# A transformer layer on one core: the output projection in one written order, its first unit and a quarter of the next inside the last attention unit, weights and operands in one pool of 4 KB tiles

## The chip, the core and the metric

The kernel runs on one core of one Trainium2 chip. The metric is the time of one execution in microseconds (us) of the device. The instructions run on five engines: TensorE (PE in the profile, with its weight loads as PEld), VectorE (DVE), ScalarE (ACT), GpSimd (POOL) and SyncE (SP), which here issues DMA transfers only.

## The reference

One layer works on 2048 tokens of 1024 features. In all projections, H = 16 heads of 64 features: 8 heads of forgetting attention ("fox") and 8 of stick-breaking attention ("sb").

```python
h = rms_norm(x, g_attn) * (1 + scale_a) + shift_a        # scale, shift, gate from silu(c) @ w_ada + b_ada
q_f, k_f, v_f, q_s, k_s, v_s, f_logit = split(h @ w_in)
o_fox = forgetting_attention(q_f, k_f, v_f, log_sigmoid(f_logit + b_fgate))
o_sb  = stick_breaking_attention(q_s, k_s, v_s)
mix = concat([head_rms_norm(o_fox, g_out_fox), head_rms_norm(o_sb, g_out_sb)])
x = x + gate_a * (mix @ w_out)                           # the output projection
h = rms_norm(x, g_mlp) * (1 + scale_m) + shift_m
u = causal_depthwise_conv(h @ w_up, conv_w, conv_b)      # the channel mixer
u_gate, u_val = split(u)
x = x + gate_m * ((silu(u_gate) * u_val) @ w_down)
return rms_norm(x, g_final)
```

`head_rms_norm` divides each head's 64 outputs of a token by their root mean square. All is float32 for the outside; the change concerns the line marked "output projection", the norm behind it, and the step into the channel mixer.

## The kernel before

**Products.** A float32 operand is split into a high and a low part (`split`: ScalarE copies the high part, L44; VectorE or GpSimd subtracts to get the low part, L45). Each product takes three matmuls, high by high, high by low, low by high.

**Attention.** It runs over 32 units (8 head pairs by 4 blocks `tb` of 512 tokens). Each unit writes its outputs, not yet normalised, to memory as `os_[p][tb]` (128 features of a head pair by 512 tokens), and the squares' sums of the heads to `var[tb]`. `interleave` puts steps of other work (the projections of later units, and `tail` in the last unit) between the steps of the unit at hand.

**Who sets the order.** A scheduler in the compiler orders each engine's instructions by its own model of their times. Two means override it: `tc.issue_after(ins)` keeps the instructions of a block behind one instruction, and `fixed()` keeps them, on every engine that it touches (the DMA issues of SyncE too), behind the last instruction of the block before, so that a chain of such blocks runs in the order in which it is written. In the output projection before, neither is used.

**Row scales.** `head_scale(tb)` takes the root and the reciprocal of `var[tb]`, transposes them on TensorE and stores them as `rstd[tb]`: one row of 512 tokens for each of the 16 heads.

**Output projection.** It runs in eight units `u` of 256 tokens (`HT`). For each of the 8 head pairs `p`, `make_mix` loads `o` (128 by 256) from `os_`, and `r`: the two rows of `rstd` that belong to the pair, each repeated to 64 partitions, by two DMAs of 64 KB (L877). GpSimd multiplies them (L880), and `split` makes the mix tile. I call this a blend. `out_proj` then computes, for each tile `t` of 128 tokens and each half `n` of the 1024 output columns, 8 × 3 = 24 matmuls (L895), adds the residual rows of `x` (L899) and stores the sum as `x1s` (L900). `finish_out` normalises the unit's two row tiles (L983), transposes them in eight steps of two (L987), applies scale and shift on ScalarE (L989) and stores the result `hf_m`, 64 DMAs of 128 KB in all, from ScalarE's queue into `hms` (L991).

Unit 0's matmuls are mixed into the last attention unit (`first_mix`, `first_out`), its sum goes to memory and is read back in the loop over `u`, which handles all units, each with the blends of the next ahead of it.

**Channel mixer.** `h_operands` reads `hms` for half of the tokens (`sblk`, 1024 tokens) in four steps `j`, and builds seven operands for a form of the product with seven multiplications in place of eight. `ob{j}` and `oa{j}` hold three and four of them in one tile each. `w_operands` does the same for the weights, and `pair_first` computes the first column tile of a token half with `j` as the outer loop, 4 × 7 × 3 = 84 matmuls (L1084); `pair` and a last piece (`REST`) follow. The whole is done for `sblk` 0, then 1; the place between them is called the change of token half. Then comes the down projection.

Of the kernel before, what the change touches and what calls it, by code (L numbers as in the profile page):

```python
# [8 lines left out]
F32 = mybir.dt.float32  # L9
# [24 lines left out]
def kernel(ctx: ExitStack, tc: tile.TileContext, x, c, w_ada, b_ada, g_attn, w_in, b_fgate,  # L34
# [17 lines left out]
    hms = [[dram.tile([P, 2 * TB], F32, name=f"hm{s}_{k}") for k in range(KT)] for s in range(2)]  # L52
# [542 lines left out]
    def weighted(o, kts, blk, V, hl, first, last, diag):  # L595
# [11 lines left out]
        for kk, kt in enumerate(kts):  # L607
            for w in range(2):
                rhs = at[:, w].rearrange("p (s q) -> p s q", q=P)[:, 0:4:3, :] if kk else at[:, w, P:3 * P]
                nc.tensor.matmul(o[:, 0:2 * P], V[kt // 4][:, kt % 4, hl, :], rhs,  # L610
                                 start=first and kk == 0 and w == 0, stop=last and kk == 1 and w == 1)
# [66 lines left out]

    deferred = []
# [8 lines left out]
    def attend(kind, p, tb, res, Fbs):  # L688
# [3 lines left out]
        oT = sb.tile([P, TB], F32, name="oT", bufs=2)  # L692
        if kind == "fox":
            ls = sx.tile([P, 2, 4], F32, name="ls", bufs=2)
        mp = p if kind == "fox" else p + 4

        def head_var(j2):
# [5 lines left out]
            def reduce():  # L703
                b = pt()
# [150 lines left out]
    HT = 2 * P  # L855

    def head_scale(tb, b, pool):
        v = var[tb].rearrange("p t h -> p (t h)")
        nc.scalar.activation(v, v, AF.Sqrt)
        nc.vector.reciprocal(v, v)  # L860
        nc.tensor.transpose(b[0:8 * NPAIR, 0:P], v, ident)
        r = pool.tile([8 * NPAIR, P], F32, name="rs", bufs=1)
# [4 lines left out]
    def load_o(u, p):  # L867
        o = p2a.tile([P, HT], F32, name="o", bufs=3)
        nc.sync.dma_start(o, os_[p][u // 2][:, (u % 2) * HT:(u % 2 + 1) * HT])
        return o  # L870

    def make_mix(u, mix, pool, loaded=()):
        for p in range(NPAIR):
            o = loaded.pop(0) if loaded else load_o(u, p)
            r = p2a.tile([P, HT], F32, name="r", bufs=2)
            for h in range(2):
                nc.sync.dma_start(r[h * HD:(h + 1) * HD],  # L877
                                  rstd[u // 2][2 * p + h:2 * p + h + 1,
                                               (u % 2) * HT:(u % 2 + 1) * HT].to_broadcast([HD, HT]))
            nc.gpsimd.tensor_mul(o, o, r)  # L880
            m = pool.tile([P, 2, HT], F32R, name="mix", bufs=8)
            split(m[:, 0], m[:, 1], o, nc.vector)
            mix.append(m)
            yield

    def out_proj(u, mix, x1_tile, acc_bank, xts):
        for t in range(2):
            row = u * HT + t * P
            xt = x1_tile()
            nc.sync.dma_start(xt, x[row:row + P, :])  # L890
            for n in range(2):
                b = acc_bank()
                for p in range(NPAIR):
                    for i, (a, bb) in enumerate(((0, 0), (0, 1), (1, 0))):
                        nc.tensor.matmul(b, mix[p][:, a, t * P:(t + 1) * P], wo[p][:, bb, n * 512:(n + 1) * 512],  # L895
                                         start=p == 0 and i == 0, stop=p == NPAIR - 1 and i == 2)
                    if p % 2:
                        yield
                nc.vector.tensor_add(xt[:, n * 512:(n + 1) * 512], b, xt[:, n * 512:(n + 1) * 512])  # L899
            nc.sync.dma_start(x1s[row // P], xt)  # L900
            xts.append(xt)
        yield

    mix0 = []

    def first_mix(loaded):
        mix = mix0
        for kt, _ in enumerate(make_mix(0, mix, p2a, loaded)):
            w = p2a.tile([P, 2, D], F32R, name=f"wo{kt}")
            nc.sync.dma_start(f(w), wos[kt])  # L910
            wo.append(w)
            yield

    def first_out():
        pair = sx.tile([P, S], F32, name="p", bufs=4)
        halves = [pair[:, :D], pair[:, D:]]
        yield from out_proj(0, mix0, lambda: halves.pop(0), lambda: bank(psc, "bc", 2), [])
# [9 lines left out]
    tail = None  # L927
    for i, u in enumerate(units):
# [12 lines left out]
        if i >= len(units) - 2:  # L941
            head_scale(i - len(units) + 2, pt(), sx)
        if nxt is None:
# [3 lines left out]
            p2a = open_pool("p2a")  # L947
            loaded = [load_o(0, p) for p in range(3)]
            wo = []
            tail = first_mix(loaded)  # L950
# [11 lines left out]
        interleave(attend(kind, p, tb, results[kind, p], Fbs), n, [(lm if i >= LATE else None, PER, False), (tail, 12, True)], follow)  # L962
# [3 lines left out]
    drain(first_out())  # L966
    tick(1 << 20)
    for t in range(2, NTB):
        head_scale(t, bank(psc, "bc", 2), p2a)
    close_pool("fx", "px", "sb", "psb")  # L970
# [4 lines left out]
    p2b = open_pool("p2b")  # L975

    NU = S // HT

    def finish_out(u, xts):
        sl = slice(u % 4 * HT, (u % 4 + 1) * HT)  # L980
        r = rms_scale(p2b, xts, "m")
        for i, xt in enumerate(xts):
            nc.vector.tensor_scalar_mul(xt, xt, r[:, i:i + 1])  # L983
        for kt in range(KT):
            ps = bank(psd, "t", 2)
            for i, xt in enumerate(xts):
                nc.tensor.transpose(ps[:, i * P:(i + 1) * P], xt[:, kt * P:(kt + 1) * P], ident)  # L987
            hf = p2b.tile([P, HT], F32, name="hf_m", bufs=2)
            nc.scalar.activation(hf, ps[:, :HT], AF.Identity, scale=mod_m[:, 0, kt:kt + 1],  # L989
                                 bias=mod_m[:, 1, kt:kt + 1])  # L990
            nc.scalar.dma_start(hms[u // 4][kt][:, sl], hf)  # L991

    def x1_tile():
        return p2b.tile([P, D], F32, name="x1", bufs=4)

    mixes = {}
    for u in range(NU):
        if u + 1 < NU:
            mixes[u + 1] = []
            drain(make_mix(u + 1, mixes[u + 1], p2b if u % 2 == 0 else p2a))  # L1000
        xts = []
        if u:
            drain(out_proj(u, mixes[u], x1_tile, lambda: bank(psd, "o", 4), xts))
        else:
            for t in range(2):
                xts.append(x1_tile())
                nc.sync.dma_start(xts[t], x1s[t])
        finish_out(u, xts)
    close_pool("p2b", "p2a")

    ho1 = open_pool("hop1")
    up_ = open_pool("up")
    NK = KT // 2
    SB = 2 * TB

    def bank_a():
        return bank(psd, "o", 4)

    def bank_c():
        return bank(psd, "t", 2)  # L1020

    obs = {}

    def h_operands(sblk, j):

        pool = ho if j == 0 else ho1
        xh = ho.tile([P, 2, SB], F32, name="xh", bufs=2)
        for i in range(2):
            nc.sync.dma_start(xh[:, i], hms[sblk][j + i * NK])
# [265 lines left out]
```

## Time and profile before

| quantity | value |
|---|---|
| median of 3 runs | 3072.32 us (3069.5 to 3076.95) |
| the profiled execution | 3060.69 us |
| its span in the profile | 3059.0 us |
| TensorE's mean granted clock in it | 0.985 of full speed |
| TensorE busy | 2950.6 us, 96% of the span, 16012 matmuls and transposes |
| VectorE, ScalarE, GpSimd busy | 2085.6, 1687.9, 969.1 us |
| DMA | 546.79 MB in 302677 packets |

The span is the time from the first to the last record of the profiled execution, which took 1.69 us more than its span. A busy time is the sum of an engine's instructions, not a measure of how well it is used. "PEclk" is the clock that the throttle granted to TensorE in a stretch (1.00 is full). In a stretch's row each engine's busy time is followed by its count of instructions. In the waits, an engine's operation stands left, what it waited for right of the arrow, then the sum of that idle time, how many waits, and the longest. L numbers are lines of the kernel.

### The profile page before, as it was taken

The page shows a single profiled execution, that of the slowest core. Times are in us where ns is not written, and L with a number is a line of the kernel's source. Part 1 is how long each engine was busy: PE and PEld are TensorE (multiplying, and loading weights), DVE is VectorE, ACT ScalarE, POOL GpSimd, SP SyncE. Part 2 cuts the span into 40 slices and gives each one's busy share as a digit, 9 for nine tenths or more (in the row PEclk, how much of TensorE's full clock was granted, in tenths as well). Part 3 has the DMA queues.
Part 4 walks back from the last instruction along what each step waited for, and adds up shares of the span by engine and source line. Part 5 has one row for each costly group of instructions (what it writes and reads, how often), then busy time and mean ns, then how long its engine had stood idle before and what let it go on. Part 6 is the DMA issues. An engine that isn't in the chain of part 4 may idle for free.

```text
span 3059.0 us, 45489 instructions
## 1 busy us (share of the span) xinstructions
PE 2950.6 (96%) x16012; PEld 2515.7 (82%) x16012; DVE 2085.6 (68%) x3190; ACT 1687.9 (55%) x3125; POOL 969.1 (32%) x983
## 2 busy tenths in 40 slices
PE   8999999999999999999999999999899998999998
PEld 7888889888988888888777688888688887888887
DVE  5787778877876567578635677778888886244243
ACT  5777777687775667578534544445444444343332
POOL 0441312151132432322123344344444442322331
PEclk8999999999999999999999999999999999999999
DMA  9758747866489864955266422222222224565562
GB/s 287 240 178 297 243 155 241 293 216 218 142 296 334 261 221 144 330 168 198 94 208 223 147 83 83 83 83 83 89 82 84 84 85 165 168 205 169 177 208 84
DMA packets 302677, 546.79 MB, mean 179 GB/s; under 512 B 30993, under 2 KB 179217, under 8 KB 301425
## 3 DMA queue, kind: packets, MB, share of 16 engines
q1 hardware_dynamic: 290928, 531.31, 52.9%
q10 hardware_dynamic: 11520, 12.59, 1.2%
q8 instruction: 126, 2.06, 0.3%
q14 instruction: 103, 0.84, 0.1%
HBM read 407.14 MB, written 130.36 MB: 176 GB/s over the span
## 4 chain that ended last, share of the span: by engine, by line
PE 35%; DVE 6%; DMA 5%; POOL 4%; issue 3%; ACT 2%; SPq 1%; ACTq 0%; POOLq 0%; DVEq 0%
PE ps_o L1084 10%; PE ps_o L1234 8%; PE ps_t L1234 4%; PE ps_t L1084 4%; PE ps_bc L1234 4%; DMA wuraw<-in_w_up_dram 2%; DMA r<-rstd 2%; DVE wu L45 2%; PE ps_pv L610 1%; PE ps_pt L601 1%; PE ps_o L895 1%; POOL ws L1072 1%; DVE u L1153 1%; POOL wuraw L1071 1%; PE ps_bc L895 1%
## 5 line engine op out<-in xcount | busy, mean ns | idle before, releaser
L1084 PE MATMUL ps_o<-oa,wu 128*128 128x512 f32 x2088 | 503.5, 392 | 11.8 <-DVE oa L45 6.0
L1084 PEld LDWEIGHTS ps_o<-oa,wu 128*128 128x128 f32 x2088 | 391.4, 188 | 100.6 <-DVE oa L45 9.8
L606 DVE TENSOR_TENSOR at<-ps_pt,at 128x512 fp32r<-128x512 f32 (+1 forms) x576 | 365.8, 652 | 100.2 <-ACT at L605 97.4
L337 PE MATMUL ps_pj<-hp,w_qk 128*128 128x512 f32 x1512 | 410.8, 403 | 12.4 <-DMA hp<-hs 9.9
L629 DVE TENSOR_TENSOR_SCAN a<-r,a 128x512 f32<-128x512 f32 (+2 forms) x320 | 367.8, 1165 | 78.6 <-ACT a L624 40.2
L610 PE MATMUL ps_pv<-at,V 128*128 128x256 f32 x2304 | 402.3, 292 | 12.4 <-ACT at L605 4.4
L605 ACT ACTIVATE at<-ps_pt 128x512 fp32r<-128x512 f32 (+1 forms) x576 | 318.7, 576 | 136.6 <-PE ps_pt L601 113.6
L610 PEld LDWEIGHTS ps_pv<-at,V 128*128 128x128 f32 x2304 | 332.8, 190 | 45.1 <-DVE at L606 13.1
L337 PEld LDWEIGHTS ps_pj<-hp,w_qk 128*128 128x128 f32 x1512 | 275.9, 190 | 69.6 <-DMA hp<-hs 13.4
L45 DVE TENSOR_TENSOR wd<-wdraw,wd 128x1024 fp32r<-128x1024 f32 x88 | 112.5, 1279 | 260.4 <-ACT wd L44 260.4
L591 PE MATMUL ps_qk<-K,Q 128*128 128x512 f32 (+2 forms) x640 | 265.5, 416 | 5.4 <-ACT a L624 3.0
L1234 PE MATMUL ps_o<-wd,g 128*128 128x512 f32 x1040 | 250.2, 390 | 8.7 <-ACT g L44 8.7
L45 POOL TENSOR_TENSOR g<-graw,g 128x512 fp32r<-128x512 f32 x84 | 141.7, 1689 | 325.4 <-ACT g L44 325.4
L44 ACT ACTIVATE wu<-wuraw 128x512 fp32r<-128x512 f32 x214 | 133.1, 626 | 198.5 <-PE ps_o L1084 150.7
L1084 PE MATMUL ps_t<-ob,wu 128*128 128x512 f32 x984 | 242.3, 391 | 0.0
L408 PE MATMUL ps_pj<-w_v,hp 128*128 128x256 f32 (+1 forms) x1536 | 237.7, 288 | 2.1 <-DVE hp L417 1.6
L1234 PEld LDWEIGHTS ps_o<-wd,g 128*128 128x128 f32 x1040 | 195.6, 188 | 49.6 <-ACT g L44 9.1
L592 PE MATMUL ps_qk<-K,Q 128*128 128x512 f32 (+2 forms) x640 | 236.3, 370 | 0.0
L408 PEld LDWEIGHTS ps_pj<-w_v,hp 128*128 128x128 f32 x1536 | 209.5, 189 | 11.1 <-DVE q L368 1.3
L1084 PEld LDWEIGHTS ps_t<-ob,wu 128*128 128x128 f32 x984 | 186.0, 189 | 39.0
L44 ACT ACTIVATE wd<-wdraw 128x1024 fp32r<-128x1024 f32 x88 | 93.0, 1057 | 210.9 <-PE ps_bc L1234 198.2
L623 ACT ACTIVATE r<-ps_qk 128x512 f32<-128x512 f32 (+2 forms) x320 | 173.1, 541 | 57.4 <-PE ps_qk L592 54.5
(231 smaller groups left out, 5517.2 us busy)
## 6 DMA issues: line engine op xcount, KB each, us to landing
hp<-hs SPq DMA_DIRECT2D x224, 512.0 KB
wuraw<-in_w_up_dram SPq DMA_DIRECT2D x84, 512.0 KB
wdraw<-in_w_down_dram SPq DMA_DIRECT2D x84, 512.0 KB
g<-u SPq DMA_DIRECT2D x42, 512.0 KB
graw<-g SPq DMA_DIRECT2D x84, 256.0 KB
hs<-hp SPq DMA_DIRECT2D x32, 512.0 KB
hp<-in_w_ada_dram SPq DMA_DIRECT2D x32, 512.0 KB
qk_fox<-q SPq DMA_DIRECT2D x32, 512.0 KB
```

Of the source, the lines that this page charges most:

```text
L44: nc.scalar.activation(hi, src, AF.Copy)
L45: (lo_engine or nc.gpsimd).tensor_sub(lo, src, f(hi))
L337: nc.tensor.matmul(acc, w[kt][:, a, n], h[:, bb], start=kt == 0 and i == 0, stop=kt == KT - 1 and i == 2)
L408: nc.tensor.matmul(av[:, t * width:(t + 1) * width], hts[kt][:, a, tok], w[1][kt][:, bb, 0:width], start=kt == 0 and m == 0, stop=kt == KT ...
L591: nc.tensor.matmul(b[:, :cw], Q[:, hl, 0, qcols], K[:, hl, :cw], start=True, stop=False)
L592: marks.append(nc.tensor.matmul(b[:, :cw], Q[:, hl, 1, qcols], K[:, hl, :cw], start=False, stop=True).ins)
L605: nc.scalar.activation(at[:, 0, lo:], b[:, lo:], AF.Copy)
L606: nc.vector.tensor_sub(at[:, 1, lo:], b[:, lo:], f(at[:, 0, lo:]))
L610: nc.tensor.matmul(o[:, 0:2 * P], V[kt // 4][:, kt % 4, hl, :], rhs, start=first and kk == 0 and w == 0, stop=last and kk == 1 and w == 1)
L629: nc.vector.tensor_tensor_scan(rev, r[:, 0:need][:, ::-1], rev, 0.0 if right[qi] is None else right[qi][:, 0:1], ALU.mult, ALU.add)
L1084: nc.tensor.matmul(b, w[:, p, j], o[:, q], start=first and i == 0, stop=last and i == 2, skip_group_check=True)
L1234: nc.tensor.matmul(banks[t][n], g[:, a, t * P:(t + 1) * P], w[:, b, n * TB:(n + 1) * TB], start=k == 0 and i == 0, stop=k == NKD - 1 and i ...
```

## The change

The arithmetic of the projection stays; its order, its tiles and its transfers change.

- Unit 0 of the projection and the first four of the 16 steps of unit 1 (a step is 6 matmuls) stand in the last attention unit. `tail_steps` gives 13 + 16 + 6 steps: eight blends of unit 0 and four of unit 1, six empty ones, and 16 of unit 0's matmuls. Unit 0's sum stays on the chip; it is stored, but not read again.
- Everything behind it stands in one written order: `chunk(u, c)` issues step `c` of unit `u`, and the table `jobs` says which other work follows that step: the blend of the next unit at every second step, the transposes and modulation of the unit before at steps 6, 8, 10, 12, the rows' sums and squares, the row scales of blocks 2 and 3, and the first operands of the channel mixer (weights and `j = 0`) during units 4 to 6.
- `r` comes by one DMA of two rows, each repeated 64 times, into 128 partitions. `fetch` issues `o` and `r` two or three blends ahead.
- The modulated rows `hf_m` are stored by SyncE, in 32 DMAs of 256 KB, into one array `hms[s]` per half of the tokens.
- The weights `wo`, mix tiles of even units and the channel mixer's operands come from one pool `big` of 20 tiles of 4 KB. Mix tiles of odd units use the channel mixer's buffers. Each of the seven operands of `h_operands` has a tile of its own, and for `sblk` 0 VectorE or GpSimd subtracts where GpSimd did.
- The last unit's end (`finish_last`) is called from `pair_first` after its second `j`.

The core of the diff, with the functions that it adds:

```diff
+    def fetch(n):
+        while len(fetched) < min(n, len(blends)):
+            u, p = blends[len(fetched)]
+            tb, sl = u // 2, slice((u % 2) * HT, (u % 2 + 1) * HT)
+            o = orp.tile([P, HT], F32, name="o", bufs=3)
+            nc.sync.dma_start(o, os_[p][tb][:, sl])
+            r = orp.tile([P, HT], F32, name="r", bufs=2)
+            nc.sync.dma_start(r, rstd[tb][2 * p:2 * p + 2, sl].rearrange("h (d n) -> h d n", d=1).to_broadcast(
+                [2, HD, HT]))
+            fetched.append((o, r))
+
+    def blend(u, p, m):
+        o, r = fetched[u * NPAIR + p]
+        nc.gpsimd.tensor_mul(o, o, r)
+        split(m[:, 0], m[:, 1], o, nc.vector)
+        mixes[u].append(m)
...
+    def out_matmuls(u, b, t, n, pp):
+        for p in (2 * pp, 2 * pp + 1):
+            for i, (a, bb) in enumerate(((0, 0), (0, 1), (1, 0))):
+                nc.tensor.matmul(b, mixes[u][p][:, a, t * P:(t + 1) * P], wo[p][n][:, bb],
+                                 start=p == 0 and i == 0, stop=p == NPAIR - 1 and i == 2)
...
-            for h in range(2):
-                nc.sync.dma_start(r[h * HD:(h + 1) * HD],
-                                  rstd[u // 2][2 * p + h:2 * p + h + 1,
-                                               (u % 2) * HT:(u % 2 + 1) * HT].to_broadcast([HD, HT]))
...
+    def big4(name):
+        return big.tile([P, 2, TB], F32R, name=name, tag="big", bufs=20)
...
+    def tail_steps():
...
         for p in range(NPAIR):
+            if p:
+                blend(0, p, next(tiles))
+            for q in range(2):
+                k, n = (2 * p + q) % NPAIR, (2 * p + q) // NPAIR
+                nc.sync.dma_start(f(wo[k][n]), wos[k][:, :, n * TB:(n + 1) * TB])
+            fetch(p + 3)
             yield
...
+        for p in range(4):
+            blend(1, p, q[:, p // 2, p % 2].rearrange("p (w n) -> p w n", w=2))
+            fetch(8 + p + 3)
+            yield
+        for _ in range(IDLE):
+            yield
         for t in range(2):
             for n in range(2):
+                b = bank(psc, "bc", 2)
+                for pp in range(4):
+                    with tc.issue_after(sums[-1]):
+                        out_matmuls(0, b, t, n, pp)
+                    yield
+                add_out(b, xts[t], n)
+            nc.sync.dma_start(x1s[t], xts[t])
...
+    class finish_out:
...
+        def modulate(self, k2, b):
+            hf = hf_tile(self.pool)
+            for k in range(2):
+                kt = 2 * k2 + k
+                nc.scalar.activation(hf[:, k], b[:, k * HT:(k + 1) * HT], AF.Identity, scale=mod_m[:, 0, kt:kt + 1],
+                                     bias=mod_m[:, 1, kt:kt + 1])
+            nc.sync.dma_start(hms[self.u // 4][:, 2 * k2:2 * k2 + 2, self.u % 4 * HT:(self.u % 4 + 1) * HT], hf)
...
+    def chunk(u, c):
+        t, n, q = ORDER.get(u, TURN)[c]
+        if (t, n) not in banks:
+            banks[t, n] = bank(psc, "bc", 2) if u == 1 and t == 0 else bank(psd, "o", 4)
+        with fixed():
+            out_matmuls(u, banks[t, n], t, n, q)
+        return t, n, q
+
+    for c in range(4):
+        with tc.issue_after(sums[2 * c - 8]):
+            chunk(1, c)
...
+    def blend_next(u, p, tiles):
+        blend(u, p, next(tiles))
+        fetch(u * NPAIR + p + 3)
...
+    job(4, 13, load_h, 0, 0)
+    job(4, 15, lambda: hgen.append(h_operands(0, nc.gpsimd)))
+    job(5, 2, load_h, 0, 1)
+    for c in range(2, 16, 2):
+        job(5, c, lambda: next(hgen[0]))
+    job(5, 6, raw_first)
+    for c in range(1, 14, 2):
+        job(6, c, split_first)
+    job(6, 2, load_h, 0, 2)
+    for u in range(1, NU):
+        if u > 1:
+            job(u, 0, rows_done, u - 1, 1)
+            job(u, 0, lambda u=u: ends[u - 1].scale())
+        if u > 1:
+            for k2 in range(4):
+                job(u, 6 + 2 * k2, lambda u=u, k2=k2: turn_rows(u - 1, k2, bank(psd, "t", 2)))
+        if u + 1 < NU:
+            job(u, 13, load_rows, u + 1)
+            if u > 1:
+                tiles = odd_tiles() if u % 2 == 0 else even_tiles()
+                for p in range(NPAIR):
+                    job(u, 2 * p, blend_next, u + 1, p, tiles)
+        job(u, 9 if u not in ORDER else 12, rows_done, u, 0)
+    for u in range(1, NU):
+        for c in range(8 if u == 1 else 0, 16):
+            t, n, q = chunk(u, c)
+            with fixed():
+                if ORDER.get(u, TURN)[c + 1:c + 2] != [(t, n, q + 1)] and (u > 1 or q in (3,)):
+                    add_out(banks.pop((t, n)), res[u][t], n)
+                for fn in jobs.get((u, c), ()):
+                    fn()
...
+    def finish_last():
+        rows_done(NU - 1, 1)
+        ends[NU - 1].scale()
+        for k2 in range(4):
+            turn_rows(NU - 1, k2, bank(psc, "bc", 2))
...
+        if sblk == 0:
+            for j in range(1, NK):
+                if j == NK - 1:
+                    load_h(0, j)
+                drain(h_operands(j, nc.vector))
+            ws = first["ws"]
+            after = finish_last
+        else:
...
+                load_h(sblk, j)
+                drain(h_operands(j, nc.gpsimd))
+                ws.extend(next(gen) for _ in range(2 if j < 3 else 1))
```

More of the change, by code (lines that the diff above doesn't have):

```diff
@@ L677, in fox_head @@
             yield
+    sums = []
     deferred = []
@@ L904 @@
[L904 to L917, printed above, removed]
+            load_res(0, t, xts[t])
@@ new lines @@
+    banks = {}
+    def chunk(u, c):
[8 more added lines that the diff above has]
+            chunk(1, c)
+    tiles = even_tiles()
+    for p in range(4, NPAIR):
+        with fixed():
+            blend(1, p, next(tiles))
+            fetch(8 + p + 3)
@@ new lines, in second_tiles, with job @@
+    def second_tiles():
+        for _ in range(2):
+            yield from halves(big4("mix"))
+        t = ho.tile([P, 2, SB], F32R, name="mixh", tag="xh", bufs=2)
+        for i in range(2):
+            yield from two(t[:, i])
+    jobs = {}
+    def job(u, c, fn, *args):
+        jobs.setdefault((u, c), []).append(lambda: fn(*args))
+    tiles = second_tiles()
+    for p in range(NPAIR):
+        job(1, 4 + p * 3 // 2, blend_next, 2, p, tiles)
+    for k2 in range(4):
+        job(1, 4 + k2, lambda k2=k2: turn_rows(0, k2, bank(psd, "t", 2)))
@@ L973 @@
+    for c in range(4, 8):
+        chunk(1, c)
+        if c == 4:
+            tick(1 << 20)
+        with fixed():
+            for fn in jobs.get((1, c), ()):
+                fn()
+    close_pool("fx", "px", "sb")
     ho = open_pool("hop0", side="right")
     wp = open_pool("wup", side="right")
[L975 to L1008, printed above, removed]
```

257 lines of the change are left out of this document (174 added, 83 removed).

## The prediction

> **What bounds the kernel now.** I read the page's first two parts, then the busy time by stretch, then the output projection's own matmuls, then the waits and the DMA queues of that stretch.
>
> ```profile
> span 3059.0 us, 45489 instructions
> PE 2950.6 (96%) x16012; PEld 2515.7 (82%) x16012; DVE 2085.6 (68%) x3190; ACT 1687.9 (55%) x3125; POOL 969.1 (32%) x983
> PE   8999999999999999999999999999899998999998
> ```
>
> TensorE sets the time: it is idle for 108 us of 3059, and the change adds and removes no matmul. What there is to win lies in its idle time and its slow matmuls, so I look at where these are.
>
> ```profile
> core 0: us, PE busy (x) PEld busy (x) DVE busy (x) ACT busy (x) POOL busy (x), PEclk, DMA share, GB/s
> 1463.00:1497.00 34.00, 31.01 (x213) 26.85 (x213) 28.36 (x73) 26.94 (x42) 2.87 (x5) 1.00 0.11 35
> 1497.00:1517.00 20.00, 18.41 (x107) 15.93 (x107) 8.53 (x16) 5.27 (x10) 0.42 (x1) 1.00 0.14 54
> 1517.00:1708.00 191.00, 176.39 (x782) 139.70 (x783) 73.90 (x123) 75.09 (x160) 55.00 (x62) 0.96 0.68 219
> 1708.00:1742.00 34.00, 27.33 (x107) 19.15 (x107) 29.88 (x29) 21.50 (x36) 15.93 (x12) 0.85 0.46 154
> 1760.00:1840.00 80.00, 80.00 (x354) 65.98 (x353) 62.50 (x73) 34.87 (x50) 34.13 (x33) 1.00 0.28 85
> 2140.00:2180.00 40.00, 31.42 (x107) 21.86 (x107) 39.03 (x41) 19.20 (x27) 17.22 (x11) 0.87 0.26 86
> 2200.00:2220.00 20.00, 17.66 (x70) 13.80 (x69) 13.89 (x16) 5.71 (x10) 8.39 (x7) 0.91 0.41 116
> ```
>
> The channel mixer (1760 to 1840) is the measure of an undisturbed TensorE: 354 matmuls of 512 columns in 80 us, 0.226 us each, clock 1.00. The output projection (1517 to 1708) and the way into the channel mixer (1708 to 1742) run with idle time and a granted clock of 0.96 and 0.85; so does the change of token half (2140 to 2180, 2200 to 2220), which has 177 matmuls in 60 us where 265 would fit: 88 too few, 20 us.
>
> ```profile
> L895 PE MATMUL ps_o<-wo,mix x672: 387/389/792, 1519.0 to 1708.1; 128*128 128x512 f32 x168
> L895 PE MATMUL ps_bc<-wo,mix x96: 387/389/500, 1438.8 to 1511.5; 128*128 128x512 f32 x96
> ...
> 1517.25 0.61 PE L706 MATMUL ps_pt<-headsel,sq 128*128 128x2 f32 x4 [1.61 <-POOL sq L701]
> ...
> 1575.42 5.05 PE L895 MATMUL ps_o<-wo,mix 128*128 128x512 f32 x21
> 1580.32 0.60 PE L987 MATMUL ps_t<-edge,x 128*128 128x128 f32 x4
> 1580.67 5.05 PE L895 MATMUL ps_o<-wo,mix 128*128 128x512 f32 x21
> ...
> 1742.44 2.88 PE L1084 MATMUL ps_o<-oa,wu 128*128 128x512 f32 x12
> ```
>
> The second row is unit 0 of the projection: it stands inside the last attention unit already. The stage I cost runs from the last attention instruction (1517.25) to the first matmul after `pair_first` (1742.44): 225.2 us. From start to start, 21 matmuls take 4.90 us, 0.233 each (1575.42 to 1580.32), and four transposes 0.35, 0.0875 each (1580.32 to 1580.67). TensorE's work in the stage: 672 × 0.233 = 156.6, 128 transposes (8 units of 16) 11.2, `pair_first` 7 × 4 × 3 = 84 matmuls, 19.6. That is 187.4 us; so 37.8 us of the stage are lost, and no written order can win more there than these and what it moves ahead of 1517.
>
> What are they lost to? The waits of the stretch from 1517 to 1742:
>
> ```profile
> POOL o L880 <- DMA r<-rstd: 92.8, 40, 6.8
> SPq L900 <- DVE x L899: 18.8, 6, 11.4
> PE ps_t L987 <- DVE x L983: 5.1, 3, 4.2
> DVE x L983 <- DMA x1s<-x: 1.3, 2, 1.2
> ```
>
> The longest is GpSimd's: the multiplication that begins each blend waits for `r`, the broadcast of the row scales. Here is its rhythm:
>
> ```profile
> 1536.01 0.74 POOL L880 TENSOR_TENSOR o<-o,r 128x256 f32<-128x256 f32 x1 [1.45 <-DMA r<-rstd]
> 1537.93 0.74 POOL L880 TENSOR_TENSOR o<-o,r 128x256 f32<-128x256 f32 x1 [1.18 <-DMA r<-rstd]
> 1538.70 1.08 SPq L877 DMA_DIRECT2D r<-rstd  x2
> 1540.08 0.74 POOL L880 TENSOR_TENSOR o<-o,r 128x256 f32<-128x256 f32 x1 [1.41 <-DMA r<-rstd]
> ```
>
> One blend each 2.0 us; a unit needs eight, 16 us, while its matmuls and transposes take 96 × 0.233 + 16 × 0.0875 = 23.8. So `r` is the slowest part of the chain that feeds TensorE, and it is hidden with 8 us to spare per unit. Whatever the change does to `r` decides more than the order does.
>
> **The change part by part.** *Unit 0 and four steps of unit 1 in the last attention unit.* Unit 0's 96 matmuls stand there now; what is new are 4 × 6 = 24, 5.6 us. TensorE is idle for 4.6 us between 1463 and 1517 (34 − 31.01 + 20 − 18.41), so they cost between 1 and 5.6 us of later attention end; I take 4, since idle time before a wait is not all usable: attention ends at 1521, and 24 × 0.233 = 5.6 us less is left after it.
>
> *The written order.* Transposes of unit u−1 stand six steps of 1.4 us behind the start of unit u, blends of u+1 at every second step. Where TensorE would stall next: at the transposes, if the scaling on VectorE is late, as in the waits above (5.1 us in three waits). VectorE's scaling waits for the store of x1, and behind it stand the subtractions of the next blends; they are due 16 steps later, 22 us. I take 5 us of stalls over seven units, bounds 0 and 14 (2 per unit).
>
> *Fewer and moved DMA issues.* The h rows go out in 32 transfers from SyncE instead of 64 from ScalarE's queue; `r` in 64 issues instead of 128; the reload of unit 0's x1 goes. SyncE issues about as much as before, and what is queued behind a waiting issue is the prefetch of `o` and `r`, two blends deep. Cost 0 while blends have 8 us to spare per unit.
>
> *The row scales in one DMA.* Now `r` comes by two DMAs whose source list is 64 repeats of one row; after, by one whose source list begins with 2 rows, then 64 repeats, into 128 partitions. Bytes and packets stay: 128 packets of 1 KB. What may change is how many of the 16 DMA engines share them.
>
> ```profile
> DMA packets 36543, 47.15 MB, mean 210 GB/s; under 512 B 4336, under 2 KB 31024, under 8 KB 36528
> ...
> q1 hardware_dynamic: 27312, 38.58, 53.7%
> q10 hardware_dynamic: 9216, 8.39, 10.9%
> ...
> hm<-hf_m ACTq DMA_DIRECT2D x64, 128.0 KB
> x<-in_x_dram SPq DMA_DIRECT2D x14, 512.0 KB
> x1s<-x SPq DMA_DIRECT2D x14, 512.0 KB
> o<-os SPq DMA_DIRECT2D x53, 128.0 KB
> r<-rstd SPq DMA_DIRECT2D x102, 64.0 KB
> xh<-hm SPq DMA_DIRECT2D x12, 512.0 KB
> wuraw<-in_w_up_dram SPq DMA_DIRECT2D x5, 512.0 KB
> ```
>
> These are the queues from 1517 to 1742. q10 carries only `hm`: 64 × 128 packets of 1 KB, in 10.9% of 16 × 225 us = 392 us, so 48 ns for a packet. On all 16 engines the new `r` takes 8 × 0.048 = 0.38 us; on two engines 64 × 0.048 = 3.07 us. Those are the ends, and no row of this trace has a list that begins with 2. I take the upper one: a transfer has to be dealt to engines along some dimension, and the outermost is the one along which the lists of all these DMAs (64, 128) are long; here it is 2. The Trainium skill says the same as a rule ("DMA: Bandwidth & Descriptors", "Rules for kernel authors"): the count of engines follows from the outermost dimension that isn't 1, and an outer dimension of c below 16 confines a DMA to at most c engines; by it `r` stands at the upper end, and no run here shows it yet.
>
> What two engines then have to do after 1521: 18 of the 64 `r` have been issued by then, so 46 × 3.07 = 141 us, and their sixteenth of all else: `hm` 8192 KB, `x` and x1 7168 each, `o` for six units 6144, six `xh` 3072 and two weight tiles 1024 make 32768 KB, 2048 per engine, at 48 ns 98 us. Together 239 us, against 648 × 0.233 + 11.2 = 162 us on TensorE. So these two engines set the pace, some 34 us per unit. After the last `r` TensorE still has 13 steps of unit 7, 18 us, while some 12 us of the 98 lie behind that `r`: the projection ends at 1521 + 239 + 18 − 12 = 1766 instead of 1708. Now the stalls of the written order are hidden.
>
> *Into the channel mixer.* The operands of its first block need only units 0 to 3, and the change builds their first quarter, the weights, and part of the rest during units 5 to 7. What follows unit 7 is `pair_first`, 19.6 us, 16 transposes 1.4, and a wait I put at 2 (bounds 0 and 8, if VectorE's 11 operations of 0.7 us for the last quarter come late): 23 us where 34 stand. It ends at 1789 instead of 1742.4: 46.6 us later.
>
> *The change of token half.* Operand tiles of 4 KB come free one by one, where now four share one tile. VectorE is busy for 39.03 of the 40 us there, and its work stays the same; it can only start earlier. I take 4 us of the 20, bounds 0 and 10.
>
> Sum: 46.6 − 4 = +42.6 us. The profiled execution took 3060.69 us, which becomes 3103.3; the median of the three runs, 3072.32, is 11.6 above it, and becomes 3115.
>
> **The rivals.** *All 16 engines share the new `r`.* Then nothing holds TensorE but its own work after 1521, 187.4 − 5.6 = 181.8 us, with 5 us of stalls and 2 on the way in: the stage ends at 1710, 32.6 us earlier than 1742.4, and 4 more come from the change of half. 3072.3 − 36.6 = 3036. For it: each row of `r` today shows 16 engines sharing; the 8 us of room per unit. Against: the list that begins with 2. It decides at one point: `r`'s landing stays under about 3 us.
>
> *Two engines, but cheaper packets.* 64 packets read the same row. If such a packet took half of the 48 ns, the two engines would have 70 + 98 = 168 us, about TensorE's 162: the projection ends at 1521 + 168 + 6 = 1695, `pair_first` at 1718, 24 us earlier than today, and with the 4 later on the time is 3044. Nothing in the rows separates these packets from others of 1 KB.
>
> *Slow `r` inside the attention too.* Twelve blends are put into the last attention unit, in order on ScalarE and VectorE, where attention's own copies stand behind them. If each takes 3.07 instead of 2.0 us, attention ends up to 12 × 1.07 = 13 us later: 3128. Against: SyncE fetches two blends ahead, and the first half of that unit has no matmuls that need them.
>
> **How the numbers follow.** Two engines without delay in the attention: 0.63; with it: 0.12; cheap packets: 0.05; sixteen engines: 0.18; 0.02 for anything between. The likeliest gives 3115; its own range, from the bounds (packets of 42 to 52 ns take 30 off or put 20 on; the change of half ±5; the way in up to +7), is 3085 to 3145. To hold 8 in 10 the range goes up to 3148 and down to 3032, which takes in the cheap packets and most of the sixteen-engine case. 0.2% is 6 us, about what a measurement of this kernel tells from no change. Faster: 0.18 + 0.05 less 0.01 for stalls larger than priced, 0.22; same 0.03, from the 0.02 in between and that 0.01; slower 0.63 + 0.12 = 0.75.
>
> **What would show it.** In the changed profile: `r` with 64 issues of 128 KB, and GpSimd's multiplications about 4 us apart instead of 2, waiting for `r`; the stretch of the projection about 245 us long with the DMA share down to some 0.4, because 14 engines wait for two; matmuls of the projection in bursts, with waits for the mix tiles and a granted clock under 0.9; `pair_first` ending near 1789. If the multiplications stay 2 us apart or less, the price of `r` is wrong, and the projection should end near 1690 with a clock of 1.00. If attention ends after 1530, slow `r` reaches into it.

## The result and the profile after

The changed kernel takes 3147.07 us (median of 4 runs, 3142.97 to 3150.17), the kernel before 3070.91 on the same chip: a ratio of 1.0245, 95% interval 1.0224 to 1.0265. The forecast was 3115, with a range up to 3148: 76 us more were measured, 43 forecast. Its profiled execution took 3142.97 us, 4 us under its median; that of the kernel before (3060.69) is 10 us under the median given here, so differences of a few us between rows of single executions count for little.

The page's first two parts, after:

```profile
span 3141.2 us, 45340 instructions
PE 2964.7 (94%) x16012; PEld 2530.7 (81%) x16012; DVE 2064.1 (66%) x3212; ACT 1681.8 (54%) x3139; POOL 948.0 (30%) x977
PE   8999999999999999997976799999899998999998
```

TensorE has the same 16012 matmuls and transposes; it is idle for 176 us instead of 108. The weak slices (7, then 7, 6, 7) are the last attention unit and the projection. The busy time by stretch (last attention unit in two parts, projection, `pair_first`; columns as in the prediction):

```profile
1420.00:1509.00 89.00, 66.57 (x386) 57.54 (x385) 57.87 (x148) 51.20 (x90) 18.20 (x30) 0.87 0.46 144
1509.00:1555.00 46.00, 44.60 (x249) 37.64 (x247) 19.61 (x41) 18.14 (x33) 3.43 (x5) 1.00 0.13 47
1555.00:1803.00 248.00, 181.54 (x762) 143.59 (x763) 79.14 (x138) 78.35 (x168) 45.12 (x55) 0.86 0.51 163
1803.00:1823.00 20.00, 20.00 (x95) 16.48 (x94) 11.48 (x19) 8.70 (x16) 1.16 (x3) 1.00 0.30 105
```

TensorE loses 22 us in the attention's part with the blends and 66 in the projection, and of these four stretches the granted clock falls, to 0.87 and 0.86, in just these two. `pair_first` runs without a gap. What TensorE stood for in the projection, first as waits summed from 1555 to 1823, then as two rows of its own timeline and the last rows of attention and projection:

```profile
POOL o L893 <- DMA r<-rstd: 143.5, 32, 9.6
DVE mix L45 <- ACT mix L44: 61.8, 18, 6.8
ACT mix L44 <- POOL o L893: 58.7, 16, 7.1
ACT mixs L44 <- POOL o L893: 48.1, 12, 6.2
PE ps_t L985 <- DVE x1u L979: 46.9, 6, 12.9
PE ps_t L985 <- DVE x1y L979: 9.3, 4, 4.2
```

```profile
1555.02 0.61 PE L709 MATMUL ps_t<-headsel,sq 128*128 128x2 f32 x4 [0.87 <-POOL sq L704]
...
1716.69 0.47 PE L985 MATMUL ps_t<-edge,x1u 128*128 128x128 f32 x1 [12.90 <-DVE x1u L979]
...
1741.74 6.66 PE L904 MATMUL ps_o<-wo,mix 128*128 128x512 f32 x21 [3.50 <-ACT mix L44]
...
1802.65 0.85 PE L1275 MATMUL ps_o<-op,wu 128*128 128x512 f32 x3
...
1823.03 5.74 PE L1275 MATMUL ps_o<-op,wu 128*128 128x512 f32 x24
```

TensorE names VectorE's scaling of a row tile (12.90 us before one transpose). But VectorE works in written order, and ahead of that scaling stand a blend's subtractions, which wait for ScalarE, which waits for GpSimd, which waits for `r` (143.5 us). One needs the whole chain of rows to see that the transposes wait for a DMA. Where the multiplications on GpSimd have nothing else in their way, their rhythm is this:

```profile
1601.18 0.73 POOL L893 TENSOR_TENSOR o<-o,r 128x256 f32<-128x256 f32 x1 [2.57 <-DMA r<-rstd]
1604.50 0.73 POOL L893 TENSOR_TENSOR o<-o,r 128x256 f32<-128x256 f32 x1 [2.59 <-DMA r<-rstd]
1607.78 0.74 POOL L893 TENSOR_TENSOR o<-o,r 128x256 f32<-128x256 f32 x1 [2.55 <-DMA o<-os]
1611.14 0.74 POOL L893 TENSOR_TENSOR o<-o,r 128x256 f32<-128x256 f32 x1 [2.62 <-DMA r<-rstd]
```

3.3 us each, where the kernel before had 2.0. For 64 packets on one engine that is 51.6 ns a packet, with whatever lies between two transfers counted in. The trace also has a record of each packet, with its start and its duration. From 1601.6 to 1603.55 us, within one `r`, there are 84 packets of 1 KB, 49.5 ns each on average, and but for short overlaps they run two at a time.

### The profile page after: what moved, and what is told of

It reads as the page before. It is cut to its first block, busy times and chain, and to the rows that moved or that the text cites. A ratio compares the mean times of both kernels' runs of the same rounds, so it can differ in the third digit from the quotient of the medians.

```text
span 3141.2 us, 45340 instructions
## 1 busy us (share of the span) xinstructions
PE 2964.7 (94%) x16012; PEld 2530.7 (81%) x16012; DVE 2064.1 (66%) x3212; ACT 1681.8 (54%) x3139; POOL 948.0 (30%) x977
## 4 chain that ended last, share of the span: by engine, by line
PE 23%; DMA 11%; DVE 9%; POOL 6%; issue 5%; ACT 3%; SPq 1%; POOLq 0%; DVEq 0%; ACTq 0%
PE ps_o L1443 8%; DMA r<-rstd 4%; PE ps_t L1443 4%; PE ps_bc L1443 4%; PE ps_o L1275 3%; DMA wuraw<-in_w_up_dram 3%; DVE wu L45 3%; DMA o<-os 2%; DVE u L1346 2%; POOL wuraw L1207 2%; POOL ws L1208 2%; POOL ws L1206 1%; PE ps_t L1275 1%; DVE u L1383 1%; PE ps_pv L610 1%
## 5 line engine op out<-in xcount | busy, mean ns | idle before, releaser
L1275 PE MATMUL ps_o<-op,wu 128*128 128x512 f32 x2592 | 613.3, 391 | 9.7 <-DVE wu L45 3.2
L1275 PEld LDWEIGHTS ps_o<-op,wu 128*128 128x128 f32 x2592 | 485.3, 188 | 118.7 <-DVE snap L1326 9.7
L610 PE MATMUL ps_pv<-at,V 128*128 128x256 f32 x2304 | 409.0, 295 | 22.0 <-ACT at L605 15.1
L605 ACT ACTIVATE at<-ps_pt 128x512 fp32r<-128x512 f32 (+1 forms) x576 | 319.0, 576 | 140.6 <-PE ps_pt L601 124.7
L610 PEld LDWEIGHTS ps_pv<-at,V 128*128 128x128 f32 x2304 | 340.3, 193 | 54.0 <-ACT at L605 17.8
L591 PE MATMUL ps_qk<-K,Q 128*128 128x512 f32 (+2 forms) x640 | 269.5, 422 | 13.7 <-DVE mn L668 5.2
L592 PE MATMUL ps_qk<-K,Q 128*128 128x512 f32 (+2 forms) x640 | 238.8, 374 | 0.0
L1275 PE MATMUL ps_t<-op,wu 128*128 128x512 f32 x888 | 222.9, 391 | 5.2 <-ACT op L44 4.4
L1275 PEld LDWEIGHTS ps_t<-op,wu 128*128 128x128 f32 x888 | 167.0, 188 | 41.9 <-ACT op L44 5.4
```

The lines of the kernel that those rows point to most:

```text
L591: nc.tensor.matmul(b[:, :cw], Q[:, hl, 0, qcols], K[:, hl, :cw], start=True, stop=False)
L592: marks.append(nc.tensor.matmul(b[:, :cw], Q[:, hl, 1, qcols], K[:, hl, :cw], start=False, stop=True).ins)
L605: nc.scalar.activation(at[:, 0, lo:], b[:, lo:], AF.Copy)
L610: m = nc.tensor.matmul(o[:, 0:2 * P], V[kt // 4][:, kt % 4, hl, :], rhs, start=first and kk == 0 and w == 0, stop=last and kk == 1 and w == 1)
L1275: nc.tensor.matmul(b, w[:, p, j], o[:, q], start=first and i == 0, stop=last and i == 2, skip_group_check=True)
```

## The experiments

Four marks divide the time of each kernel: the last row-sum matmul of the attention (its end), the last addition of `pair_first` in both halves of the tokens (L1111 before, L1304 after), and the first matmul of the down projection. "Last unit" is counted from the row-sum matmul near 1345 us. The four stretches are read from the one profiled execution of each kernel (`a_copies8` and `a8_again`, the same kernel, differ by up to 1.2 us in a stretch); medians and ratios to the kernel before come from all runs, in which that kernel's median was 3065.46 to 3070.91.

| kernel | median | ratio, 95% interval | last unit | to first half | first to second half | to down projection |
|---|---|---|---|---|---|---|
| before | 3067.46 | | 171.7 | 229.3 | 428.9 | 402.5 |
| changed | 3147.07 | 1.0245 (1.0224–1.0265) | 204.9 | 271.5 | 436.6 | 396.4 |
| b_one | 3161.74 | 1.0311 (1.0288–1.0334) | 181.7 | 317.7 | 430.7 | 402.9 |
| a_two | 3053.79 | 0.9959 (0.9941–0.9977) | 179.5 | 203.7 | 439.3 | 396.4 |
| a_copies2 | 3077.76 | 1.0032 (1.0020–1.0045) | 191.3 | 215.8 | 436.9 | 396.3 |
| a_copies4 | 3053.54 | 0.9952 (0.9936–0.9969) | 184.5 | 202.3 | 438.6 | 396.3 |
| a_copies8 | 3049.27 | 0.9938 (0.9921–0.9954) | 181.8 | 199.3 | 436.9 | 396.8 |
| a_fast12 | 3126.29 | 1.0198 (1.0179–1.0216) | 183.4 | 273.6 | 439.3 | 395.9 |
| a8_again | 3050.22 | 0.9950 (0.9932–0.9969) | 182.2 | 200.5 | 437.6 | 395.7 |
| a8_hvec | 3046.70 | 0.9937 (0.9921–0.9953) | 182.5 | 199.8 | 433.6 | 399.0 |
| a8_idle0 | 3050.51 | 0.9952 (0.9937–0.9966) | 181.4 | 200.4 | 440.9 | 396.7 |

**a_two: the changed kernel with the old form of `r`.**

```diff
-            nc.sync.dma_start(r, rstd[tb][2 * p:2 * p + 2, sl].rearrange("h (d n) -> h d n", d=1).to_broadcast(
-                [2, HD, HT]))
+            for h in range(2):
+                nc.sync.dma_start(r[h * HD:(h + 1) * HD], rstd[tb][2 * p + h:2 * p + h + 1, sl].to_broadcast([HD, HT]))
```

> The changed kernel with the row scales fetched as before: two DMAs of 64 partitions, one row each, all else as changed. Theory (two DMA engines carry the one-DMA form and set the pace): multiplications on GpSimd at most 2.0 us apart, attention ends near 1525 instead of 1555, the stage from there to the end of pair_first falls from 268 to about 190 us, the time to 3036 to 3050. Rival (the written order itself costs the time: in-order queues let transposes wait for a scaling that stands behind blends; the form of r is incidental): 3130 to 3147, the waits of the transposes for VectorE stay at some 50 us.

Measured: 3053.79. This one edit takes back the whole loss and 14 us more. The stretch from the attention's end to the first half falls from 271.5 to 203.7 us, the last unit from 204.9 to 179.5. The transposes' waits for VectorE fall from 56.2 us (`x1u` and `x1y`) to 13.6. The theory holds in its main point and the rival falls, but the theory's sizes are missed: the time is 4 us above its range, the attention ends at 1531.0 instead of 1525, and the stretch behind it is some 10 us longer than the 190. The multiplications aren't at most 2.0 us apart either: 27 of them from 1537.5 to 1618.2 us are 3.1 apart on average, about what TensorE takes for an eighth of a unit (23.8 / 8 = 3.0). SyncE issues 64 transfers more than with eight copies (below), and the two kernels' intervals overlap.

**b_one: the kernel before with the new form of `r`.**

```diff
-            for h in range(2):
-                nc.sync.dma_start(r[h * HD:(h + 1) * HD],
-                                  rstd[u // 2][2 * p + h:2 * p + h + 1,
-                                               (u % 2) * HT:(u % 2 + 1) * HT].to_broadcast([HD, HT]))
+            nc.sync.dma_start(r, rstd[u // 2][2 * p:2 * p + 2, (u % 2) * HT:(u % 2 + 1) * HT].rearrange(
+                "h (d n) -> h d n", d=1).to_broadcast([2, HD, HT]))
```

> The kernel before with the changed form of r alone: one DMA of two rows, each repeated 64 times. Theory: blends 3.3 us apart where nothing else is in the way, more beside other transfers; two engines have about 51 x 3.3 + 98 = 266 us of work in a projection of 191 us, so the time rises by 55 to 80 us, to 3125 to 3150. Rival (written order): 3071, within 6 us; half as many issues on SyncE could even give a little back.

Measured: 3161.74, above the range of 3125 to 3150. The form of `r` alone makes the old kernel slower than the changed one. The count of 51 holds. What the range had no term for is the attention, which ends 10 us later:

```profile
L706 PE MATMUL ps_pt<-headsel,sq x256: 165/251/272, 128.1 to 1527.5; 128*128 128x2 f32 x128
...
L876 SPq DMA_DIRECT2D r<-rstd x51: 482/509/937, 1539.1 to 1761.0; - x51
```

The last row sum stands at 1527.5, against 1517.6 in the kernel before, and 51 fetches lie behind it. From the first of them to the last multiplication of a blend it takes 232.6 us (1539.1 to 1771.7) where the kernel before took 150.0 (1530.0 to 1680.0). These 82.6 us are above the forecast 55 to 80 by themselves; the rest of the way to the first half takes 6.6 us more.

**a_copies2, a_copies4, a_copies8: one DMA, but a longer list.** Each row of the scales is stored 2, 4 or 8 times, so that the source list of the one DMA begins with 4, 8 or 16 rows, each repeated 32, 16 or 8 times. The 128 packets of 1 KB stay. With eight copies:

```diff
-    rstd = [dram.tile([2 * NPAIR, TB], F32, name=f"rstd{t}") for t in range(NTB)]
+    rstd = [dram.tile([2 * NPAIR, 8, TB], F32, name=f"rstd{t}") for t in range(NTB)]
...
-            nc.sync.dma_start(rstd[tb][:, t * P:(t + 1) * P], r[2 * NPAIR * t:2 * NPAIR * (t + 1)])
+            nc.sync.dma_start(rstd[tb][:, :, t * P:(t + 1) * P],
+                              r[2 * NPAIR * t:2 * NPAIR * (t + 1)].rearrange("h (c n) -> h c n", c=1).to_broadcast([2 * NPAIR, 8, P]))
...
-            nc.sync.dma_start(r, rstd[tb][2 * p:2 * p + 2, sl].rearrange("h (d n) -> h d n", d=1).to_broadcast(
-                [2, HD, HT]))
+            rows = rstd[tb][2 * p:2 * p + 2, :, sl].rearrange("h c n -> (h c) n")
+            nc.sync.dma_start(r, rows.rearrange("h (d n) -> h d n", d=1).to_broadcast([2 * 8, HD // 8, HT]))
```

> The changed kernel with each row of the scales stored eight times; r is still one DMA of 128 packets of 1 KB, its source list now begins with 16 rows, each repeated 8 times. Theory (the first length of the list sets the count of engines): 16 engines, blends at most 2.0 us apart, time within 8 us of the two-DMA form. Rival A (written order): 3130 to 3147. Rival B (it is the one DMA that is slow, through its single issue or through many readers of one row, not the count of engines): 3110 to 3147.

> As with eight copies, but each row stored twice: the list begins with 4 rows, each repeated 32 times. Theory: 4 engines, r takes 32 x 0.0516 = 1.65 us; their work after the attention is 46 x 1.65 + 98 = 174 us against 162 us of matmuls and transposes: blends between 1.7 and 3 us apart, time 0 to 20 us above the kernel with eight copies. Rival B (one DMA as such): 3110 to 3147, no difference between two and eight copies.

> The changed kernel with each row of the scales stored four times: the list begins with 8 rows, each repeated 16 times. Theory (the engines that carry r have r's packets and their sixteenth of all other transfers to do; what costs time is only the part of that above TensorE's work): 8 engines have 46 x 16 x 0.0516 + 98 = 136 us to do behind the attention against 162 us of TensorE, so nothing is left of the delay: 3050, between 3043 and 3057, the same as with 16 engines. Rival (each halving of the engines costs in proportion to the time of one r, whatever else runs): the 28 us between 4 and 16 engines go with 1.65 - 0.41 us per r, so 8 engines with 0.83 us stand 9 us above 16 engines, near 3059.

Measured with a list that begins with 2, 4, 8, 16: 3147, 3078, 3054, 3049. One DMA as such isn't slow (rival B falls: with 16 rows it is as fast as two DMAs), and many readers of one row are not either: in `a_two`, 64 packets of each DMA read the same row. What remains is the first length of the list. The packet records show how many packets run at once. In the projection of the changed kernel exactly two packets are in flight for 81 of 248 us; with a list that begins with 4 it is four packets for 29 of 192 us, with 8 eight for 10 of 178. Apart from that the commonest count in flight is 16 in each of them, and also with a list that begins with 16. `a_copies2` stands 28 us above eight copies, beyond the 0 to 20 expected: 9.5 of it in the last attention unit, which the sum of 174 against 162 us did not cover, and 16.5 behind it. `a_copies4` stands 4 us above eight copies with intervals that overlap, 3 us by the stretch to the first half; the theory had 0, the rival 9, so it leans to the theory but doesn't settle it. Blends at most 2.0 us apart were expected here too, and again they come at TensorE's pace (3.1 us apart from 1538.6 to 1619.5). The stretches of the kernel with eight copies (last attention unit, projection, `pair_first`):

```profile
1421.00:1533.00 112.00, 104.22 (x636) 88.10 (x634) 77.83 (x189) 69.00 (x123) 22.24 (x35) 0.98 0.45 138
1533.00:1712.00 179.00, 170.29 (x778) 138.55 (x777) 87.41 (x141) 80.78 (x171) 49.18 (x56) 0.96 0.72 228
1712.00:1732.00 20.00, 20.00 (x95) 16.51 (x94) 11.52 (x20) 9.34 (x19) 1.29 (x1) 1.00 0.34 119
```

The same work as in the changed kernel, with the DMA engines' mean share at 0.72 instead of 0.51 and the clock at 0.96: a mean share of 0.51 was 14 engines waiting for two.

**a_fast12: fast row scales in the last attention unit alone.**

```diff
+            if len(fetched) < 12:
+                for h in range(2):
+                    nc.sync.dma_start(r[h * HD:(h + 1) * HD], rstd[tb][2 * p + h:2 * p + h + 1, sl].to_broadcast([HD, HT]))
+            else:
+                nc.sync.dma_start(r, rstd[tb][2 * p:2 * p + 2, sl].rearrange("h (d n) -> h d n", d=1).to_broadcast(
+                    [2, HD, HT]))
```

> The changed kernel with the first twelve pairs of row scales (those of the blends in the last attention unit) fetched by two DMAs of 64 partitions, all later ones by one DMA as changed. Theory (slow row scales cost twice: in the last attention unit, where attention's own copies stand behind the blends' copies on ScalarE, and in the projection behind it): attention ends near 1531 as with fast row scales everywhere, instead of 1555, and the 270 us behind it stay, so 3147 - 24 = 3123, between 3115 and 3132. Rival (the last attention unit is late through its 24 new matmuls and four new blends alone): attention still ends near 1550 and the time is 3140 to 3150.

Measured: 3126.29, the attention's end at 1534.4. The two costs are separate and add up: 204.9 − 183.4 = 21.5 us in the attention, 273.6 − 199.3 = 74.3 behind it, 96 together, against 98 between 3147 and 3049. How a row scale reaches attention shows in the changed kernel's waits from 1420 to 1555, in TensorE's rows, and in two rows of ScalarE:

```profile
POOL o L893 <- DMA r<-rstd: 43.7, 11, 6.2
ACT mix L44 <- POOL o L893: 21.8, 8, 5.1
```

```profile
1451.87 0.55 PE L591 MATMUL ps_qk<-K,Q 128*128 128x512 f32 x1 [3.66 <-DVE mn L668]
1459.19 0.58 PE L610 MATMUL ps_pv<-at,V 128*128 128x256 f32 x1 [3.30 <-ACT at L605]
1474.25 0.58 PE L610 MATMUL ps_pv<-at,V 128*128 128x256 f32 x1 [4.52 <-ACT at L605]
```

```profile
1456.68 0.42 ACT L44 ACTIVATE mix<-o 128x256 fp32r<-128x256 f32 x1 [4.97 <-POOL o L893]
1458.56 1.06 ACT L605 ACTIVATE at<-ps_pt 128x512 fp32r<-128x512 f32 x2
```

`at` L605 is attention's own copy on ScalarE. It comes late because a blend's copy ahead of it on that engine waits for GpSimd: 4.97 us in the first of ScalarE's rows, ahead of TensorE's late matmul at 1459.19, and 21.8 us in all.

**a8_again, a8_hvec, a8_idle0: what else eight copies leave.** The first is `a_copies8` unchanged, to compare on one chip. `a8_hvec` lets VectorE do the subtractions of the second half's operands; `a8_idle0` drops the six empty steps.

```diff
-                drain(h_operands(j, nc.gpsimd))
+                drain(h_operands(j, nc.vector))
```

```diff
-    IDLE = 6
+    IDLE = 0
```

> The kernel with eight copies of each row again, unchanged, to compare the next two with it on one chip: 3049, between 3043 and 3055.

> The kernel with eight copies, and at the change of token half the two subtractions of each operand step by VectorE instead of GpSimd (an argument of one call). Theory (VectorE, busy for 29.9 of 30 us there, is slowed by GpSimd: its subtraction of 128x512 takes 0.68 us alone and up to 1.78 beside one of GpSimd): eight subtractions more, 8 x 0.68 = 5.4 us, against some 12 operations 1.1 us faster, 13 us, so 3 to 8 us less than with eight copies. Rival (VectorE's own count of operations is the bound): 4 to 6 us more.

> The kernel with eight copies and no empty steps between the blends and unit 0's matmuls in the last attention unit, so that the blends spread over 12 of 29 steps instead of 12 of 35. Theory (what is left of the attention's delay, some 4 us beyond its 24 new matmuls, is VectorE, busy 52 of 60 us where the blends lie and 22 of 47 behind): attention ends 2 to 4 us earlier, 0 to 4 us less than with eight copies. Rival (matmuls that come sooner wait for blends, the transfers of the weights lie closer together): 2 to 6 us more.

Measured: 3050.22, 3046.70, 3050.51. `a8_idle0`: the last unit is 0.8 us shorter, not 2 to 4, and the time is the same; where the blends lie among the steps isn't what holds the attention. `a8_hvec`: the way to the second half is 4.0 us shorter, that to the down projection 3.3 longer, and the totals' intervals overlap. The medians differ by 3.5 us, at the low end of the theory's 3 to 8, and the rival's rise of 4 to 6 us isn't there. Inconclusive as to the time.

## Why the prediction was right, and where not

**The row scales: right, in mechanism and size.** The prediction's price of an `r` was 64 × 48 ns = 3.07 us; measured 3.3. The Trainium skill's rule ("DMA: Bandwidth & Descriptors", "Rules for kernel authors": the outermost length of a list caps the count of engines) agrees with the series over 2, 4, 8 and 16 and with the packets in flight. Which of the 16 engines carried a packet the records don't say. The sum over two engines (46 fetches and a sixteenth of all else, 239 us) can be checked against the transfers from 1555 to 1803:

```profile
hm<-hf_m SPq DMA_DIRECT2D x28, 256.0 KB
o<-os SPq DMA_DIRECT2D x45, 128.0 KB
r<-rstd SPq DMA_DIRECT2D x45, 128.0 KB
xh<-hm SPq DMA_DIRECT2D x8, 512.0 KB
x1y<-in_x_dram SPq DMA_DIRECT2D x7, 512.0 KB
x1u<-in_x_dram SPq DMA_DIRECT2D x7, 512.0 KB
x1s<-x1y SPq DMA_DIRECT2D x7, 512.0 KB
x1s<-x1u SPq DMA_DIRECT2D x6, 512.0 KB
wuraw<-in_w_up_dram SPq DMA_DIRECT2D x5, 512.0 KB
```

Without `r` these are 33,408 KB, 2088 per engine, 100 us at 48 ns per KB; with 46 × 3.3 = 152 us that makes 252, and the stretch is 248 us long. With the 18 − 12 = 6 us that the prediction adds for the time around the last `r` it would be 258, so at 3.3 us per `r` the sum is some 10 us too high; that the total came out closer is in part luck. From the attention's end to the end of `pair_first` the prediction had 1789 − 1521 = 268 us; measured 1823.0 − 1555.0 = 268.0. That part of the sum stands, and so do its signs: a clock under 0.9 and a low DMA share (0.51, where some 0.4 was forecast). The 268 hides two differences that cancel: the projection took 247.6 us (245 forecast), the way into the channel mixer 20.4 (23). One sign failed: the waits were to be for the mix tiles, but TensorE waited only 9.2 us for these and 56.2 at the transposes for VectorE's scaling, the stalls that the prediction called hidden. Whether more than two `r` buffers would have helped was not tried; the packet records speak against it, since fewer than two packets are in flight for only 13 of the 248 us.

**The attention: the step that failed.** The prediction moved the blends into the last attention unit at 4 us and gave slow `r` inside the attention, with at most 13 us, a chance of 0.12 as a rival. That rival came true, with its sign (an attention end after 1530), and its price was mis-sized: 21.5 us. It took the rhythm of `r` alone (12 × 1.07 us). But in that stretch the projection's weights come in, and a sixteenth of them goes through each of the same two engines. The transfers from 1420 to 1509, and some of GpSimd's blends there:

```profile
wo<-wos SPq DMA_DIRECT2D x16, 512.0 KB
...
o<-os SPq DMA_DIRECT2D x12, 128.0 KB
```

```profile
1426.70 0.72 POOL L893 TENSOR_TENSOR o<-o,r 128x256 f32<-128x256 f32 x1 [6.21 <-DMA r<-rstd]
...
1449.51 0.72 POOL L893 TENSOR_TENSOR o<-o,r 128x256 f32<-128x256 f32 x1 [5.49 <-DMA r<-rstd]
1455.93 0.72 POOL L893 TENSOR_TENSOR o<-o,r 128x256 f32<-128x256 f32 x1 [5.45 <-DMA r<-rstd]
1462.19 0.73 POOL L893 TENSOR_TENSOR o<-o,r 128x256 f32<-128x256 f32 x1 [4.61 <-DMA r<-rstd]
1468.38 0.73 POOL L893 TENSOR_TENSOR o<-o,r 128x256 f32<-128x256 f32 x1 [5.46 <-DMA r<-rstd]
...
1499.49 0.74 POOL L893 TENSOR_TENSOR o<-o,r 128x256 f32<-128x256 f32 x1 [2.57 <-DVE at L606]
```

Some 6 us a blend from 1449.5 to 1468.4, not 3.07, and 5.2 on average. From the first blend (1426.7) to the fifteenth (1499.5) two engines have 14 × 3.3 us of `r`, and (8192 + 1536) / 16 = 608 KB of weights and `o` at 48 ns, 29 us: 75 us, measured 72.8. In the packet records exactly two packets are in flight for 33 of the 89 us from 1420 to 1509. The load of two engines was summed for the projection and not for the attention, where the same sum was due. The other 11.7 us of the unit's 33.2 stay with fast row scales (about 10 by eight copies): 5.6 are the 24 matmuls at 0.233 us each, at the upper bound of the range given for them; the rest has no shown cause. The 4.6 us by which the changed kernel is late before that unit were in no step; the other kernels made from the changed one show 2.5 to 6.9 there, `b_one` none.

**Into the channel mixer: right.** 23 us forecast, 20.4 measured from 1802.65 to 1823.03, without the wait of 2 us.

**The change of token half: wrong.** Forecast −4 us; measured 436.6 − 428.9 = +7.7 before it and 396.4 − 402.5 = −6.1 behind it. Part of both figures is only the place of the mark, ahead of which stand 17 more matmuls of 512 columns than before (1828 against 1811), 3.8 us at 0.226; what counts is the net of +1.6 us. The later stall is gone, the first is not. VectorE is busy there throughout (29.90 of 30 us), which fits that tiles that come free sooner bring nothing, but no run separates this from other causes:

```profile
2230.00:2260.00 30.00, 22.30 (x82) 16.55 (x83) 29.90 (x34) 13.20 (x21) 17.82 (x11) 0.89 0.27 85
```

The errors add up to the miss: 33.8 us at the attention's end, 5.6 in the halves, nothing between. That makes 39.4 us; the span grew by 82.2 us, 39.6 more than the 42.6 forecast.

**The range held by luck.** 3147.07 lies 0.9 us inside its upper end of 3148, and outside the 3085 to 3145 of the case that the prediction held likeliest. (The bounds that it names for that case, added straight, give 3080 to 3147.) Yet 33.8 of the 39.4 us come from the attention, for which the likeliest case had 4 us and the rival at 3128 up to 13 more, and none of the bounds added there is for it.

**The rival with 16 engines** was put at 3036, 36 us below the kernel before; with eight copies it measures 18 below. Three terms were off: the attention's end (15.6 us late instead of 4), the halves (+2.3 instead of −4), and the stretch to the first half, which fell by 30 us, not 36. So the change without its slow `r` is worth some 14 us (two DMAs) to 18 us (eight copies) by the medians, and that one line hid it.

## What to carry to other kernels

A broadcast that is merged into fewer DMAs can become slower at the same bytes and packets: look at the first length of its list, and at how long it takes on that many engines together with their share of all other transfers, in every stage where it is used. When a transfer in a written order slows, the wait shows on engines that have nothing to do with it; follow the waits back engine by engine until one names a DMA. A small load that hides in one stage has to be priced again where the change moves it.

## What the runs showed of the hardware

A packet is no cheaper when 64 of them read the same row: 49.5 ns for 1 KB by the packet records of the changed kernel (84 packets), against 46.9 for the 8192 stores of 1 KB from ScalarE's queue in the kernel before.

At the change of token half (eight copies) VectorE's subtraction of 128x512 takes 0.68 us alone and 1.78 beside one of GpSimd:

```profile
2119.67 0.68 DVE L45 TENSOR_TENSOR op<-xh,op 128x512 fp32r<-128x512 f32 x1
2119.89 1.61 POOL L1213 TENSOR_TENSOR wuraw<-wuraw,ws 128x512 f32<-128x512 f32 x1
2120.27 1.78 DVE L45 TENSOR_TENSOR op<-tt,op 128x512 fp32r<-128x512 f32 x1
2121.46 1.74 POOL L1170 TENSOR_TENSOR xh<-xh 128x512 f32<-128x512 f32 x1
2121.97 1.78 DVE L45 TENSOR_TENSOR op<-xh,op 128x512 fp32r<-128x512 f32 x1
2123.67 0.68 DVE L1175 TENSOR_TENSOR tt<-xh 128x512 f32<-128x512 f32 x1
```

The Trainium skill ("SBUF — State Buffer", "Who interferes with whom") says that a VectorE instruction with two inputs in SBUF contends with a GpSimd instruction that reads SBUF. These rows agree. In `a8_hvec`, where VectorE takes over subtractions of GpSimd, VectorE's 16 subtractions `op<-xh` from 2100 to 2180 us take 0.75 us on average instead of 0.95 (`a8_again`), and the time moved by no more than its interval.
